# A GeGLU MLP kernel: in the two down phases that make w_down operands, block loads moved ahead of the transposes of x, and their first sums moved later

## The chip, the cores and the metric

One NeuronCore of a Trainium2 chip runs the whole kernel. The metric is the device time of one execution in microseconds (us). Most executions agree within 0.3%. Profiles are of one execution each.

## The reference, cut to what matters

```python
gate = x @ w_gate                       # x: 8 x 1024 x 1024, weights 1024 x 4096
up = x @ w_up
gate = 0.5 * gate * (1 + np.tanh(np.sqrt(2 / np.pi) * (gate + 0.044715 * gate ** 3)))
h = gate * up
return (h @ w_down).astype(np.float32)  # w_down: 4096 x 1024
```

## The kernel before

The kernel works in 8 passes of 1024 tokens, numbered 0 to 7. Each has a gate/up phase and a down phase. The first passes use a Strassen-like scheme with 7 products (P1 to P7), the later ones a deeper one with 24 operands, whose w_down combinations are made once, in "units", beside other work, and stored in DRAM. The down phases of passes 2 and 3 carry two units each. A down phase of this kind has 14 chunks of w_down operands, 1 MB each, and 4 groups of rows per chunk: 56 *slots* of 8 matmuls, numbered from 0. A unit reads *blocks* of w_down, 256 KB each, sums and scales them, and stores the results.

In the profiles TensorE is PE (the matmuls), VectorE is DVE (here the sums), ScalarE is ACT (here copies and scaled copies); SyncE (SP) and GpSimd (POOL) issue DMA transfers. PSUM is the memory in banks that takes the matmuls' sums; the *ring* holds the chunks on the core. A transfer *lands* when its data has arrived. The *granted clock* is the share of TensorE's full clock that the profile reports. The parts that matter:

```python
def down(p):
    ...
    steps = {}
    if p in UNITS_DOWN:                       # passes 2 and 3, two units each
        free = deque(xc[:, j * 512 : (j + 1) * 512] for j in range(24, 38))   # 14 buffers
        for i, u in enumerate(UNITS_DOWN[p]):
            load, fs = wd_unit(u, xc[:, i * 8192 : i * 8192 + 4096], free)
            steps[i] = [load]                 # 3 loads on SyncE, 1 casting load on GpSimd
            for k, f in enumerate(fs):        # 20 steps: store, sum (VectorE), scaled copy (ScalarE)
                steps.setdefault(3 + 19 * i + k, []).append(f)
    ...
    for v, name in enumerate(DSEQ):           # P1 P2 P6 P5 P7 P3 P4
        for nb in range(2):
            kc = 2 * v + nb                   # chunk
            dc = d_chunk(p, kc)
            for g in range(G):                # slot (2 * v + nb) * 4 + g
                for n in range(8):
                    nc.tensor.matmul(ps_all[:, bank[b, g]], lhs[:, j, g * P : (g + 1) * P], dc[:, n, :], ...)
                ...
                if nb == 1:
                    if name == "P1":          # slots 4 to 7: P2 adds to this copy from slot 8
                        bank["c", g] = ps_free.popleft()
                        nc.scalar.copy(ps_all[:, bank["c", g]], ps_all[:, bank["a", g]])
                    ...
                for s in sums.get((name, nb, g), ()):
                    hsum(*s)
                ...
                if nb == 0 and g == 0 and p + 1 < NPASS:
                    ...
                    if v == (2 if p < FAST - 1 else 0):
                        transpose_x(p + 1)    # four DMA transposes on SyncE's queue
                for f in steps.get((2 * v + nb) * G + g, ()):
                    f()
                ...
            if kc == 0 and p < FAST:          # FAST is 3: in pass 2, not in pass 3
                for k in range(3, 6):
                    load_d(p, k)              # chunks 3, 4, 5, on SyncE
            load_d(p, kc + 6)
```

In the timelines SyncE issues its DMAs in program order (in pass 2 before the change: transposes at 796.08 us, blocks at 811.92, chunks at 815.36). Chunks 0 to 2 of pass 2, and 0 to 5 of pass 3, are issued during the gate/up phase.

## Time and profile before

| | |
|---|---|
| time, median of the first 3 runs | 2293.49 us (2290.92 to 2293.87) |
| TensorE busy | 2257.8 us of 2289.5 us |
| TensorE waits for the PSUM copy, passes 2 and 3 | 9.9 + 8.3 us |
| down phase of pass 0, pass 2, pass 3 | 96.7, 108.3, 106.8 us |

The core's time is the sum of TensorE's phases, one after the other. A phase's length against the 96.7 us that its 448 matmuls take without a wait tells what it loses. The prediction below shows the lines.

### The profile page before, as it was taken

Reading aid. Unit: us, or ns where it says so; the run is one execution under the profiler, and the core shown is the slowest. Engines: PE = TensorE matmul, PEld = TensorE weight load, DVE = VectorE, ACT = ScalarE, POOL = GpSimd, SP = SyncE. Lnnn points to the kernel's source line nnn. Section 1 sums busy time; section 2 is a strip of 40 time slices with the busy share of each in tenths; the row PEclk is TensorE's granted clock in tenths of the full one; section 3 lists DMA queues with packets and bytes.
Section 4 is the critical chain, followed back from the end, with each engine's and each line's share of the span. In section 5 each row is a group of like instructions: output and inputs, shape, how many; then the busy total and the mean of one; then the engine's idle time right before and its main releaser. Section 6 shows DMA issues by size and latency. Waiting matters only on the chain.

```text
span 2289.5 us, 42138 instructions
## 1 busy us (share of the span) xinstructions
PE 2257.8 (99%) x16255; PEld 1589.1 (69%) x16255; DVE 1524.7 (67%) x2170; ACT 959.3 (42%) x1876; POOL 687.8 (30%) x826
## 2 busy tenths in 40 slices
PE   9999999999999989999899999999999999999999
PEld 4444444444444435888358888888888888888888
DVE  5576368772587744877548777766776767866674
ACT  4443135551355522665216651255503554045520
POOL 1342013230133300555105541154502544034520
PEclk9999999999999999999999999999999999999999
DMA  9998959888899999998989999998999989998876
GB/s 239 175 210 209 252 145 223 216 255 248 184 220 223 265 301 300 326 379 294 290 270 326 389 323 305 333 304 291 300 321 320 319 275 305 332 312 275 285 287 231
DMA packets 305306, 632.98 MB, mean 276 GB/s; under 512 B 78992, under 2 KB 181392, under 8 KB 285840
## 3 DMA queue, kind: packets, MB, share of 16 engines
q1 hardware_dynamic: 250048, 556.88, 71.3%
q0 software_dynamic: 55056, 73.41, 19.3%
q8 instruction: 127, 2.08, 0.4%
q14 instruction: 75, 0.61, 0.1%
HBM read 565.18 MB, written 138.41 MB: 307 GB/s over the span
## 4 chain that ended last, share of the span: by engine, by line
PE 93%; DMA 3%; DVE 2%; SPq 1%; issue 1%; ACT 0%; DVEq 0%; ACTq 0%
PE ps L827 38%; PE ps L620 22%; PE ps L965 16%; PE ps L1079 16%; DMA ring<-w_ops 1%; DVE ring L349 1%; SPq L254 1%; DMA h_s<-wd_ops 1%; PE ps L1178 1%; DVE x_sums L277 0%; DMA x_sums<-wd_ops 0%; DVE tmp L639 0%; DMA h_a<-in_x_dram 0%; DVE h_a L657 0%; DVE h_s L410 0%
## 5 line engine op out<-in xcount | busy, mean ns | idle before, releaser
L827 PEld LDWEIGHTS <-ring 128*128 128x128 f16 x8320 | 814.1, 98 | 97.8 <-issue 3.2
L804 POOL TENSOR_TENSOR h_a<-tmp 128x256 f16<-128x256 f32 x640 | 472.5, 758 | 787.3 <-ACT tmp L792 774.6
L827 PE MATMUL ps<-x_sums,ring 128*128 128x256 f16 x5760 | 655.9, 273 | 0.2 <-DVE tmp L789 0.2
L789 DVE TENSOR_TENSOR tmp<-tmp,ps 128x512 f32<-128x512 f32 x640 | 414.4, 683 | 147.7 <-PE ps L827 103.3
L620 PEld LDWEIGHTS <-ring 128*128 128x128 f16 x2632 | 257.5, 98 | 314.8 <-issue 5.1
L774 ACT COPY tmp<-ps 128x512 f32<-128x512 f32 x520 | 303.5, 585 | 219.6 <-PE ps L827 146.6
L620 PE MATMUL ps<-x_sums,ring 128*128 128x512 f16 x1504 | 341.1, 379 | 3.1 <-DVE ring L349 1.7
L792 ACT ACTIVATE tmp<-tmp 128x256 f32<-128x256 f32 x640 | 263.3, 417 | 175.6 <-DVE tmp L787 81.6
L965 PE MATMUL ps<-ring,h_a 128*128 128x512 f16 x1408 | 308.9, 382 | 18.2 <-ACT ps L981 18.2
L827 PE MATMUL ps<-x_b,ring 128*128 128x256 f16 x2560 | 305.9, 273 | 2.5 <-DVE tmp L789 2.5
L965 PEld LDWEIGHTS <-h_a 128*128 128x128 f16 x1536 | 150.9, 98 | 202.0 <-issue 22.8
L646 POOL TENSOR_TENSOR h_a<-tmp 128x512 f16<-128x512 f32 x94 | 148.9, 1584 | 377.4 <-ACT tmp L644 288.4
L787 DVE TENSOR_TENSOR tmp<-ps,tmp 128x512 f32<-128x512 f32 x240 | 165.4, 689 | 143.0 <-ACT tmp L774 98.7
L620 PE MATMUL ps<-x_b,ring 128*128 128x512 f16 x1128 | 259.1, 379 | 0.0
L639 DVE TENSOR_TENSOR tmp<-ps,tmp 128x512 f32<-128x512 f32 x188 | 127.1, 684 | 135.6 <-ACT tmp L631 132.7
L1079 PEld LDWEIGHTS <-h_a 128*128 128x128 f16 x1792 | 175.4, 98 | 20.3
L1079 PE MATMUL ps<-ring,h_a 128*128 128x256 f16 x1536 | 172.9, 273 | 0.0
L1136 ACT ACTIVATE tmp<-ps 128x512 f32<-128x512 f32 x48 | 28.2, 597 | 290.1 <-PE ps L1079 219.7
L893 ACT ACTIVATE tmp<-ps 128x512 f32<-128x512 f32 x64 | 38.2, 597 | 265.9 <-PE ps L965 265.9
L631 ACT COPY tmp<-ps 128x512 f32<-128x512 f32 x188 | 110.1, 586 | 91.8 <-PE ps L620 89.3
L349 DVE TENSOR_TENSOR ring<-ring 128x1024 f16<-128x1024 f16 x188 | 132.8, 721 | 7.2 <-PE ps L965 3.8
L644 ACT ACTIVATE tmp<-tmp 128x512 f32<-128x512 f32 x94 | 58.8, 626 | 147.5 <-DVE tmp L639 147.4
(94 smaller groups left out, 1557.5 us busy)
## 6 DMA issues: line engine op xcount, KB each, us to landing
ring<-w_ops SPq DMA_DIRECT2D x480, 512.0 KB, 5.1
ring<-wd_quads SPq DMA_DIRECT2D x88, 1024.0 KB, 7.3
ring<-wd_ops SPq DMA_DIRECT2D x49, 1024.0 KB, 7.8
out_dram<-tmp SPq DMA_DIRECT2D x128, 256.0 KB, 6.2
w_ops<-x_sums SPq DMA_DIRECT2D x110, 256.0 KB, 6.2
ring<-in_w_gate_dram POOLq DMA_DIRECT2D x23, 1024.0 KB, 9.1
ring<-in_w_up_dram POOLq DMA_DIRECT2D x23, 1024.0 KB, 17.3
w_ops<-h_s SPq DMA_DIRECT2D x82, 256.0 KB, 5.1
```

What stands on the lines that cost most here:

```text
L349: nc.vector.tensor_tensor(o, a, b, op)
L620: nc.tensor.matmul(ps(b, w), lhs[:, k], rhs[:, k, :], start=(first and k == 0), stop=(k == KH - 1), skip_group_check=True,)
L639: nc.vector.tensor_tensor(o, ps("b", w), o, ADD)
L646: nc.gpsimd.tensor_tensor(hq[TO[n]][:, i, :], tmp[:, t[n, 1]], tmp[:, t[n, 0]], MUL)
L774: nc.scalar.copy(tmp[:, t[o[1]]], ps_all[:, bank[o[2]]])
L787: nc.vector.tensor_tensor(d, b, a, SUB)
L789: nc.vector.tensor_tensor(d, a, b, ADD if o[4] == "add" else SUB)
L792: nc.scalar.activation(d, d, GELU, scale=GSC)
L804: nc.gpsimd.tensor_tensor(h, tmp[:, t[o[1]], MQ : 2 * MQ], g, MUL)
L827: nc.tensor.matmul(ps_all[:, bank[c], w * MQ : (w + 1) * MQ], lhs[:, w, k], rhs[:, k], start=(first and w == 0 and k == 0), stop=(k == KH ...
L965: nc.tensor.matmul(ps_all[:, bank[b, g]], lhs[:, j, g * P : (g + 1) * P], dc[:, n, :], start=(first and j == 0), stop=(j == NP - 1), skip_ ...
L1079: nc.tensor.matmul(ps_all[:, bank[c], m * MQ : (m + 1) * MQ], lhs[:, j, m * P : (m + 1) * P], rhs[:, j, :], start=(first and j == 0 and m ...
```

## The change

The intent is that the unit's blocks are there when ScalarE's first scaled copy asks for them, and that this copy stands behind the PSUM copies in any case.

```diff
                 load, fs = wd_unit(u, xc[:, i * 8192 : i * 8192 + 4096], free)
-                steps[i] = [load]
+                steps.setdefault(0, []).append(load)
                 for k, f in enumerate(fs):
-                    steps.setdefault(3 + 19 * i + k, []).append(f)
+
+                    steps.setdefault(9 + (17 if i else 0) + 5 * k // 6, []).append(f)
...
                     for s in sums.get((name, nb, g), ()):
                         hsum(*s)
+                    for f in steps.get((2 * v + nb) * G + g, ()):
+                        f()
                     if p == 0:
...
                             transpose_x(p + 1)
-                    for f in steps.get((2 * v + nb) * G + g, ()):
-                        f()
```

## The prediction

> **What bounds the kernel now.** I read the page first. The third line below names the instruction groups that carry the chain.
>
> ```profile
> PE 2257.8 (99%) x16255; PEld 1589.1 (69%) x16255; DVE 1524.7 (67%) x2170; ACT 959.3 (42%) x1876; POOL 687.8 (30%) x826
> ...
> PE 93%; DMA 3%; DVE 2%; SPq 1%; issue 1%; ACT 0%; DVEq 0%; ACTq 0%
> PE ps L827 38%; PE ps L620 22%; PE ps L965 16%; PE ps L1079 16%; DMA ring<-w_ops 1%; DVE ring L349 1%; SPq L254 1%; DMA h_s<-wd_ops 1%; PE ps L1178 1%; DVE x_sums L277 0%; DMA x_sums<-wd_ops 0%; DVE tmp L639 0%; DMA h_a<-in_x_dram 0%; DVE h_a L657 0%; DVE h_s L410 0%
> ```
>
> TensorE is busy 99% of 2289.5 us. This change removes no matmul, so it can pay only through the 1% in which TensorE waits. The view of waits, for TensorE alone, shows how that splits; columns are total, times, longest:
>
> ```profile
> PE ps L965 <- ACT ps L981: 18.2, 2, 9.9
> PE ps L827 <- DVE tmp L789: 2.7, 3, 1.4
> PE ps L620 <- DVE ring L349: 1.7, 4, 0.4
> ```
>
> One line dominates: two waits in the down matmuls (L965), for the copy by ScalarE of a partial sum from one PSUM bank to another (L981). Two waits, and two phases that make w_down operands (passes 2 and 3): that is what the change is after. The chain in order of time (start, length, what) gives the phases' lengths. The first line is pass 0's down phase, with none of this work; the next three are from pass 2, the last two from pass 3:
>
> ```profile
> 213.73 96.69 PE ps L965 x448
> ...
> 796.00 13.83 PE ps L965 x64
> ...
> 819.10 0.59 ACT ps L981
> 819.73 84.60 PE ps L965 x384
> ...
> 1109.44 0.49 ACT ps L981
> 1109.98 84.54 PE ps L965 x384
> ```
>
> A clean phase is 448 matmuls in 96.69 us: 56 steps ("slots") of 8 matmuls, 1.727 us each. Pass 2 takes 904.32 (where the next phase's piece starts) - 796.00 = 108.32 us, 11.6 over clean. Pass 3 takes 1194.52 - 1087.73 (its first down matmul in the timeline) = 106.79, 10.1 over. Together 21.7 us, 0.95% of the time: the ceiling of the change.
>
> Why ScalarE is late, from the timeline of pass 2 (start, length, engine, line; the bracket is the idle time before it and what ended it):
>
> ```profile
> 796.08 15.79 SPq L254 DMA_TRANSPOSE x_b<-x_half  x4
> ...
> 811.92 3.33 SPq L470 DMA_DIRECT2D x_sums<-wd_ops  x6
> 815.36 2.51 SPq L529 DMA_DIRECT2D ring<-wd_ops  x4
> ...
> 818.56 0.63 ACT L500 ACTIVATE x_sums<-x_sums 128x512 f16<-128x512 f16 x1 [21.69 <-DMA x_sums<-wd_ops]
> ...
> 819.10 1.55 ACT L981 COPY ps<-ps 128x512 f32<-128x512 f32 x3
> 819.73 10.57 PE L965 MATMUL ps<-ring,h_a 128*128 128x512 f16 x41 [9.91 <-ACT ps L981]
> ```
>
> SyncE's one queue issues the four transposes of x for 15.8 us, then the loads of w_down blocks. In ScalarE's order, the first scaled copy of a block (L500, slot 3) stands ahead of the PSUM copies (L981, slots 4 to 7), so they wait for its load and TensorE for them. Windows of 4 us show a second cost (PE busy is the second number; granted clock follows POOL):
>
> ```profile
> 812.00:816.00 4.00, 0.00 (x0) 0.00 (x0) 0.57 (x2) 0.00 (x0) 0.00 (x0) 0.58 1.10 220
> ...
> 820.00:824.00 4.00, 4.00 (x13) 1.52 (x12) 4.00 (x7) 2.24 (x5) 0.00 (x0) 0.64 1.00 421
> 824.00:828.00 4.00, 4.00 (x21) 1.79 (x19) 3.97 (x7) 0.00 (x0) 0.00 (x0) 1.00 1.02 424
> ```
>
> After the wait TensorE restarts at half clock (13 matmuls in 4 us, then 21). So pass 2's excess is 9.9 of wait + 1.7 of slow restart, pass 3's 8.3 + 1.8.
>
> **What the Trainium skill says.** "TensorE: Matmul & The Clock Gate" (Part 1, The two states you'll see): the clock falls to half after an idle window of about 3.4 us and returns after about as long busy. Here it fell about 2.8 us after TensorE stopped at 809.8 (full until about 812.6) and was back at about 823, 3.2 us after the restart; it agrees roughly. The same page (Architectural detail) calls ScalarE a strict FIFO, as the trace shows: ready copies sat behind L500. "Perfetto Trace Analysis" (Summary: the profiler window per engine type) says a DMA's profiled interval on a hardware queue is its issue and hides the data movement; so I add the landing time. Here the six loads issue in 3.3 us and land 3.4 to 7.4 us after issue.
>
> **The change part by part.** It adds and removes no work; it reorders.
>
> (a) Both units' loads (six on SyncE, 3.3 us to issue; two casting loads on GpSimd) now go ahead of the transposes. SyncE reaches them at 796.1; the last is issued at about 799.4 and lands within 7.4 us, by about 807.
>
> (b) The first sums and scaled copies move from slot 3 to slot 9. In ScalarE's order all four PSUM copies (slots 4 to 7) now come first. I compared the instruction orders: in the two phases L981 is x4 with nothing between. Slot 9 ends some 17 us into the phase, about 813, after the loads. Both causes of the two waits are removed: -11.6 and -10.1.
>
> (c) The transposes move back by the loads' 3.3 us. Whatever follows them on SyncE keeps its time: it still stands behind 15.8 + 3.3 us of issue. In pass 2 that is L529: w_down chunks 3, 4, 5 and 6 of the down phase itself. Chunk 3 is first read in slot 12. Before, TensorE reached slot 12 late, at 819.73 + 6.9 = 826.6, and chunk 3 (issued 815.36, landed 8.9 us later) was there at 824.3: 2.3 us to spare. The old wait covered this one. Now TensorE reaches slot 12 at 795.84 + 12 x 1.727 = 816.6, and chunk 3 is still issued at 796.08 + 3.3 + 15.8 + gaps = 815.3. Its landing should be quicker, with no block loads in front: in pass 1 a chunk issued right after the transposes landed 6.0 us later (a different stretch of the schedule, but the same 1 MB). So 821.3, and a new wait of about 4.7 us. That is longer than the 2.8 us at which the clock fell, so add 1.7 for a slow restart: 6.4 us. Chunk 4 follows some 2.5 us later (before, chunks 3 and 4 landed 2.5 us apart) and is needed a further 6.9 us on: no wait. Pass 2 keeps 11.6 - 6.4 = 5.2.
>
> (d) In pass 3 chunks 0 to 5 are issued during gate/up, the last at 1087.9, before the transposes. Only chunk 6 comes behind them (1105.84 before), needed in slot 24, at 1087.7 + 41.4 = 1129. No new wait: pass 3 keeps 10.1.
>
> (e) The second unit's 20 steps now take slots 26 to 41 rather than 22 to 41: 1.2 sums per slot. A sum is 0.43 us on VectorE; that is 0.1 us more per slot. VectorE idled 7.1 us (pass 2) and 13.7 us (pass 3) just before the add at slot 36 that frees a bank for slot 40. Covered.
>
> Sum: -5.2 - 10.1 = -15.3 us; 2293.5 - 15.3 = 2278.
>
> **The rivals.**
> 1. Everything is recovered, 21.7 us: 2272. For it: the two waits are the only large ones. Against: chunk 3. The transposes would have to issue in 10 us rather than 15.8; other passes show 13.1 to 19.7.
> 2. The chunk wait eats pass 2's whole gain: 2283. It needs a wait of 10 us. The 1.5 MB of block loads now lie in the queue ahead of the transposes and could slow them by some us, and with 19.7 us of transposes, as in pass 0, chunk 3 lands at 825.2. Half plausible.
> 3. Contention later: denser stores stop VectorE on its 14 buffers until the add of slot 36 is late. Pass 2 has 16.5 us of waits on those stores in VectorE, yet none reached TensorE. It would cost 2 to 5 us: 2281 to 2283.
> 4. Transposes too late for the scaling and sums of x from slot 32: they land at about 820, slot 32 comes after 851. Ruled out.
>
> **Range and chances.** The floor is 2272, the likely mishaps end near 2284, and the three runs of before spread over 3 us: 2271 to 2284 holds it 8 times in 10. A gain over 2% (46 us) is twice the ceiling: 0.01. A loss over 2% would need a new wait of 46 us plus the gain: 0.005.
>
> **What would show it.** Right: the waits of L965 for L981 are gone; the pass 3 phase is about 97 us; in pass 2 one TensorE wait of 3 to 7 us at slot 12, 21 us into the phase, for the DMA into the ring (or put down to "issue"), and a dip in granted clock after it; the phase some 103 us. Wrong: no TensorE gap at slot 12 (rival 1), one near 10 us (2), or gaps around slot 40 (3). A pass 3 phase well over 97 us would mean that I missed a load there.

## The result, and the profile after

The changed kernel takes 2277.94 us (median of 4 runs, 2275.76 to 2280.97); before, in the rounds of the same comparison, 2292.20 us. The ratio is 0.9939, interval 0.9922 to 0.9956: 0.6% faster. Added lines move line numbers by one: L966 is the down matmul that was L965, L982 the PSUM copy that was L981.

TensorE's largest wait in the changed kernel (total, times, longest); the next is 1.7 us in total:

```profile
PE ps L966 <- DMA ring<-wd_ops: 5.4, 1, 5.4
```

The 18.2 us of waits for ScalarE are gone. In their place stands one wait of 5.4 us for a load of w_down operands into the ring. The chain in order of time says where:

```profile
795.30 13.83 PE ps L966 x64
...
814.84 6.54 DMA ring<-wd_ops
...
821.42 77.77 PE ps L966 x352
899.19 54.16 PE ps L827 x496
...
1082.96 96.69 PE ps L966 x448
```

Pass 2's phase is 899.19 - 795.30 = 103.9 us, 7.2 over clean, where it was 11.6 over. Pass 3's is one piece of 96.69 us. The gain of the two phases is 4.4 + 10.1 = 14.5 us; the medians differ by 14.3, the two profiled spans (2289.5 and 2273.7) by 15.8. The timeline of pass 2 shows the order of events:

```profile
795.37 3.52 SPq L470 DMA_DIRECT2D x_sums<-wd_ops  x6
...
798.99 15.75 SPq L254 DMA_TRANSPOSE x_b<-x_half  x4
...
803.97 0.57 ACT L982 COPY ps<-ps 128x512 f32<-128x512 f32 x1 [7.80 <-PE ps L966]
...
809.64 1.15 ACT L500 ACTIVATE x_sums<-x_sums 128x512 f16<-128x512 f16 x2
...
814.84 3.14 SPq L529 DMA_DIRECT2D ring<-wd_ops  x5
...
821.42 8.91 PE L966 MATMUL ps<-ring,h_a 128*128 128x512 f16 x33 [5.40 <-DMA ring<-wd_ops]
```

The PSUM copies run as soon as TensorE has their sums, and the first scaled copies come after the fourth of them. The ring loads (L529) still stand behind the transposes, at 814.84, and slot 12, which TensorE reaches at 816.0, needs the first of them. Windows of 2 us show the half clock after the wait (second number PE busy; the granted clock is the third from the end):

```profile
820.00:822.00 2.00, 0.58 (x2) 0.25 (x2) 0.00 (x0) 0.00 (x0) 0.00 (x0) 0.83 1.00 422
822.00:824.00 2.00, 2.00 (x7) 0.65 (x5) 0.00 (x0) 0.00 (x0) 0.00 (x0) 0.50 1.02 430
824.00:826.00 2.00, 2.00 (x9) 0.82 (x8) 0.00 (x0) 0.60 (x1) 0.00 (x0) 0.81 1.00 422
```

It costs 7.2 - 5.4 = 1.8 us. One more line, from the waits of pass 2's down phase: VectorE now waits longer for free buffers, 30.4 us against 16.5, but no TensorE wait came from it.

```profile
DVE x_sums L277 <- DMA wd_quads<-x_sums: 30.4, 8, 14.9
```

### The profile page after: what moved, and what is told of

Read it like the earlier page. It is cut to its first block, busy times and chain, and to the rows that moved or that the text cites. A ratio compares the mean times of both kernels' runs of the same rounds, so it can differ in the third digit from the quotient of the medians.

```text
span 2273.7 us, 42142 instructions
## 1 busy us (share of the span) xinstructions
PE 2255.4 (99%) x16255; PEld 1587.4 (70%) x16255; DVE 1522.1 (67%) x2170; ACT 959.7 (42%) x1876; POOL 688.1 (30%) x826
## 4 chain that ended last, share of the span: by engine, by line
PE 94%; DMA 3%; DVE 2%; issue 0%; SPq 0%; ACT 0%; DVEq 0%; ACTq 0%
PE ps L827 37%; PE ps L620 23%; PE ps L966 17%; PE ps L1080 16%; DMA ring<-w_ops 2%; DMA h_s<-wd_ops 1%; PE ps L1179 1%; DVE ring L349 1%; DMA h_a<-in_x_dram 0%; DMA ring<-wd_ops 0%; DVE x_sums L277 0%; SPq L254 0%; DVE tmp L639 0%; DVE h_a L657 0%; DVE h_s L410 0%
## 5 line engine op out<-in xcount | busy, mean ns | idle before, releaser
L966 PE MATMUL ps<-ring,h_a 128*128 128x512 f16 x1408 | 307.3, 381 | 5.4 <-DMA ring<-wd_ops 5.4
L966 PEld LDWEIGHTS <-h_a 128*128 128x128 f16 x1536 | 150.5, 98 | 188.0 <-issue 7.9
```

## The experiments

The theory: all that the two phases lost, before and after, comes from what stands behind the 15 us of transposes on SyncE's queue. Before, that was the block loads; the wait for them also hid that the chunk loads of pass 2 were late. Eight runs were made in two groups of five rounds, four in each; all gave correct results. The first group holds the two halves of the change and the first tries of chunks first, on either kernel; the second holds the changed kernel again, chunks first again, and the two runs with later transposes. Each group shares its runs of the kernel before, and the groups ran on different chips (13 and 4 in the record). The kernel before took 2293.72 us (median of 11 runs) in the first group and 2291.87 in the second, so across groups the ratios are to be compared, not the times.

**The loads alone.** The changed kernel with the sums back in their old slots:

```diff
-                    steps.setdefault(9 + (17 if i else 0) + 5 * k // 6, []).append(f)
+                    steps.setdefault(3 + 19 * i + k, []).append(f)
```

> Half of the change alone: the block loads go ahead of the transposes of x, but the sums keep their old slots (3 to 22 and 22 to 41), so the first scaled copy still stands ahead of the PSUM copies on ScalarE. My theory (the copy waited for the late load, not for its place in the order as such): the block it reads is issued about 1 us into the phase and lands some 5 us later, about when the copy's turn comes (slot 3, 5 to 7 us in), so the PSUM copies are in time for slot 8 at 13.8 us: no wait of the down matmuls for ScalarE, the pass 3 phase is 97 us, pass 2 again has its wait of 5 to 6 us for chunk 3 in slot 12 and takes about 104 us. Time about 2278 us, ratio to before 0.9935 to 0.9945, as the whole change. Rival (the place in ScalarE's order is what counts): waits of several us for the PSUM copies remain in both phases, and the time lies between 2283 and 2292 us.

Measured: 2278.90 us, ratio 0.9939 (0.9924 to 0.9953). TensorE's waits have the same single large line (5.5 us for the ring load), pass 2's phase is 900.57 - 795.86 = 104.7 us, pass 3's 96.69. ScalarE in pass 2:

```profile
802.51 0.63 ACT L500 ACTIVATE x_sums<-x_sums 128x512 f16<-128x512 f16 x1 [5.78 <-DMA x_sums<-wd_ops]
804.53 0.57 ACT L982 COPY ps<-ps 128x512 f32<-128x512 f32 x1 [1.39 <-PE ps L966]
```

The scaled copy still stands first and still waits for its load, but the load comes in time: the PSUM copy then waits for TensorE, not TensorE for it. With the blocks early, the place in the order alone did no harm.

**The late sums alone.** The kernel before with only the slots changed; the loads stay behind the transposes:

```diff
-                    steps.setdefault(3 + 19 * i + k, []).append(f)
+                    steps.setdefault(9 + (17 if i else 0) + 5 * k // 6, []).append(f)
```

> The other half alone: the sums come at slots 9 to 24 and 26 to 41, but the block loads stay behind the transposes. My theory: the PSUM copies now stand ahead of the late scaled copy, so the waits for ScalarE go; the pass 3 phase is 97 us. In pass 2 the chunk loads still stand behind the transposes and now also behind the six block loads, so chunk 3 lands about 8.9 us after its issue at 19.5 us into the phase, 28.4 us in, against 20.7 us needed: a wait of 7 to 8 us for it in slot 12, 2 us more than in the whole change; the phase is about 106 us. Time about 2280 to 2281 us, ratio 0.9945 to 0.9955. Rival (late blocks now stop VectorE before the sums of h that the products of slot 16 read): a second wait in slot 16, in pass 3 too, and a time of 2284 us or more.

Measured: 2279.83 us, ratio 0.9946 (0.9932 to 0.9961). The waits for ScalarE are gone here too: the PSUM copies now run before the scaled copy, whose load is as late as before. ScalarE in pass 2, and the chain of this kernel:

```profile
805.79 0.57 ACT L981 COPY ps<-ps 128x512 f32<-128x512 f32 x1 [7.80 <-PE ps L965]
...
818.03 1.15 ACT L500 ACTIVATE x_sums<-x_sums 128x512 f16<-128x512 f16 x2 [6.49 <-DMA x_sums<-wd_ops]
```

```profile
797.12 13.83 PE ps L965 x64
...
815.61 8.36 DMA ring<-wd_ops
...
824.01 77.61 PE ps L965 x352
901.62 52.41 PE ps L827 x480
...
1087.33 96.69 PE ps L965 x448
```

The chunk takes 8.36 us to land, behind the six block loads, against 6.54 in the changed kernel; 8.9 was expected. The wait is only 6.2 us, less than the 7 to 8 expected: the chunk was issued some 18.5 us after the phase's start, not 19.5, since the transposes issued in 14.2 us. Pass 2's phase is 104.5 us, pass 3's 96.69, and no wait came at slot 16. So either half of the change removes both waits; the two gains are not added but are the same gain. The times of the halves cannot be told from the whole: the intervals overlap.

**The changed kernel again**, as the control of the second group (chunks first again, and the two runs with later transposes):

> The changed kernel again, as the control in the same rounds as the next three. Expected as recorded: about 2278 us, ratio to before 0.992 to 0.9955, pass 2's down phase 103 to 105 us with one wait of 5 to 6 us for chunk 3, pass 3's 96.7 us. If the profiles differ elsewhere, it is in the stretch before pass 2's down phase, where runs of the same schedule have differed by up to 3 us.

Measured: 2279.47 us, ratio 0.9942 (0.9930 to 0.9954). Its profile has a chunk wait of 6.2 us, where 5 to 6 were expected, a pass 2 phase of 900.36 - 794.48 = 105.9 us, somewhat over the 103 to 105 expected, and a pass 3 phase of 96.69. The slow restart cost more here: 352 matmuls took 78.92 us where clean they take 352 x 0.2158 = 75.97, so 2.9 us against 1.8. The windows show why; the clock was at half for longer:

```profile
824.00:826.00 2.00, 2.00 (x6) 0.69 (x5) 0.00 (x0) 0.60 (x1) 0.00 (x0) 0.50 1.01 426
826.00:828.00 2.00, 2.00 (x8) 0.83 (x7) 0.00 (x0) 0.12 (x1) 0.00 (x0) 0.72 1.01 360
```

**Chunks 3 to 5 ahead of the transposes, on the changed kernel.**

```diff
                 if nb == 0 and g == 0 and p + 1 < NPASS:
...
+                    if v == 0 and p == FAST - 1:
+                        for k in range(3, 6):
+                            load_d(p, k)
                     if v == (2 if p < FAST - 1 else 0):
                         transpose_x(p + 1)
...
-            if kc == 0 and p < FAST:
+            if kc == 0 and p < FAST - 1:
```

> The whole change, and in pass 2 the loads of chunks 3, 4 and 5 are issued ahead of the transposes as well. My theory (chunk 3's place behind the transposes is all that is left of the loss): the wait in slot 12 goes, the granted clock does not dip in the phase, and the pass 2 phase is 96.7 to 97.5 us against 103.9 in the changed kernel. Time 2270 to 2272 us, ratio 0.990 to 0.991; faster than the changed kernel by 6 to 7 us. Rival (the wait only moves, since transposes that now stand behind 3 MB more of loads hold up the operand stores and chunk 6 behind them): a new wait at slot 24 or at the start of pass 3's gate/up, and no more than 3 us gained over the changed kernel.

Measured: 2274.41 us, ratio 0.9915 (0.9901 to 0.9930). Pass 2's phase is one piece, free of waits, so the wait is removed and did not move:

```profile
798.05 96.69 PE ps L966 x448
```

In the same rounds this is 4.5 us below the loads alone, whose profile lost 8.0 us in pass 2. But the time was some 3 us over what was expected, and the phase had started 2.7 us later than in the changed kernel's profile. So it ran again beside the control:

> The changed kernel with chunks 3 to 5 of pass 2 ahead of the transposes, again: its first profile had a pass 2 phase of 96.7 us with no wait, but its time was only 3.5 us below that of the changed kernel (in other rounds), where 7 were expected; the profile had started that phase 2.7 us later. My theory (that delay is scatter of the executions and not of the kernel): in the same rounds as the control it is 5 to 8 us faster than the changed kernel, about 2271 to 2272 us, and the pass 2 phase does not start later than the control's by more than 1 us. Rival (the change costs something elsewhere): again only 2 to 4 us faster, with 2 us or more lost in the gate/up phase after it.

Measured: 2270.14 us, ratio 0.9901 (0.9889 to 0.9914), 9.3 us below the control's median. The phase started at 794.96, 0.5 us after the control's. The later start of the first try was thus not the kernel's doing: up to there the programs of all ten profiles are the same, and this phase starts between 794.5 and 798.1 us in them. Whether the chip or the execution made it late is not settled; three of the first try's four runs took 2274.4 to 2274.6 us, so it was not one stray execution. The gain over the control is larger than the 5 to 8 expected, since this control's profile lost 9.2 us in pass 2 rather than 7. TensorE's timeline in that phase (the bracket is the wait before a piece):

```profile
794.80 55.42 PE L966 MATMUL ps<-ring,h_a 128*128 128x512 f16 x256
...
866.59 26.06 PE L966 MATMUL ps<-ring,h_a 128*128 128x512 f16 x120 [0.84 <-DVE tmp L897]
```

A small wait is new: 0.84 us just after slot 40, for VectorE's add (L897). VectorE had stood waiting for buffers in front of it. The first try did not have it.

**Chunks 3 to 5 ahead of the transposes, on the kernel before.** The same edit without the change:

> The kernel before, with only the loads of chunks 3, 4 and 5 of pass 2 put ahead of the transposes. My theory (before the change, chunk 3's lateness was hidden behind the wait for ScalarE): no gain at all; the block loads come 1 to 2 us later, so the wait for the PSUM copies in pass 2 grows from 9.9 to about 11 to 12 us. Time 2292 to 2296 us, ratio 0.999 to 1.002. Rival (chunk 3 was already part of the loss in the kernel before): the pass 2 phase gets shorter by 2 us or more and the time falls below 2290 us.

Measured: 2298.32 us, ratio 1.0021 (1.0006 to 1.0035), slightly slower, and above the 2292 to 2296 expected. SyncE's timeline, and the waits:

```profile
795.44 1.59 SPq L529 DMA_DIRECT2D ring<-wd_ops  x3
797.14 18.64 SPq L254 DMA_TRANSPOSE x_b<-x_half  x4
815.82 2.96 SPq L470 DMA_DIRECT2D x_sums<-wd_ops  x6
```
```profile
PE ps L965 <- ACT ps L981: 23.1, 2, 14.2
```

The block loads came some 4.5 us later in the phase, not 1 to 2, because the transposes took 18.6 us to issue behind the chunk loads; the wait in pass 2 grew from 9.9 to 14.2 us and not to 12. The edit that gained 4.5 to 9.3 us with the blocks early gains nothing on the kernel before. It is not a clean test of chunk 3 there, since it also delayed the blocks, which is enough to explain the loss (4.3 us more wait in pass 2, 4.6 us by the medians). That chunk 3 did not bind the kernel before is read from its waits: in pass 2 TensorE waited only for the copies.

**The transposes later, on the kernel before.** One thing is moved, and the sums keep their slots:

```diff
-                    if v == (2 if p < FAST - 1 else 0):
+                    if v == (2 if p < FAST - 1 else 0) and p not in UNITS_DOWN:
                         transpose_x(p + 1)
+                if v == 0 and nb == 1 and g == 0 and p in UNITS_DOWN and p + 1 < NPASS:
+                    transpose_x(p + 1)
```

> The kernel before with one thing moved: in passes 2 and 3 the transposes are issued from slot 4 on, behind the block loads and the chunk loads; the sums keep their old slots. My theory (all that was lost in the two phases was lost to the transposes' 15 us ahead of the loads on one queue): both phases take 96.7 to 98 us, no wait for ScalarE and none for chunk 3, and the time is 2270 to 2273 us, ratio 0.990 to 0.9915, some 6 us better than the changed kernel. Rival (the sums at their old slots, now with early blocks and stores held up behind the transposes, run out of buffers and stop VectorE or ScalarE): a wait at slot 16 or later of 2 us or more in each phase, and a time above 2275 us.

Measured: 2272.29 us, ratio 0.9912 (0.9899 to 0.9925). There is no wait in either phase, and each takes 96.69 us; pass 2's in the chain, and SyncE's order in its timeline:

```profile
795.53 96.69 PE ps L965 x448
```
```profile
795.60 3.59 SPq L470 DMA_DIRECT2D x_sums<-wd_ops  x6
799.30 3.49 SPq L529 DMA_DIRECT2D ring<-wd_ops  x4
803.18 21.32 SPq L254 DMA_TRANSPOSE x_b<-x_half  x4
```

This is the theory's plainest test: nothing but the transposes moved, and all of the two phases' loss went (19.6 us by the medians, of the 21.7 counted). They now take 21.3 us to issue in pass 2, and no TensorE wait in the phase comes from it.

**The transposes later, on the changed kernel.** The same edit on top of the change:

> The changed kernel with the transposes issued from slot 4 on in passes 2 and 3: block loads, chunk loads, then the transposes, and the late sums. My theory: as the run with chunks 3 to 5 first, both phases 96.7 us, 2270 to 2273 us, and within 1.5 us of the kernel before with only the transposes moved: the late sums add nothing once the loads are early. Rival (the late sums matter once the stores stand behind the transposes): 2 us or more faster than the one with old slots.

Measured: 2273.15 us (2267.74 to 2277.53), ratio 0.9912 (0.9898 to 0.9927), the same ratio as without the late sums. Its profile has a wait of 1.1 us for L897 in pass 2, as in the second run of chunks 3 to 5 first; pass 3's phase is 96.69. No gain from the late sums is seen once the loads are early; the intervals are too wide to exclude one of 2 us. With chunks first the median was lowest, 2270.14 us, but its interval overlaps with those of these two; which of the three is best is not settled.

## Why the prediction was right

The prediction was 2278 us and the result 2277.94. Step by step:

- **(a) and (b), the two waits go.** Right. No wait for L982 is left, and either half alone does it; the prediction named both parts together and did not see that one is enough.
- **(c), the new wait in slot 12 of pass 2.** Right in place and cause. Chunk 3 was issued 19.7 us into the phase (814.84 - 795.14), predicted 19.5. It landed in 6.5 us, predicted 6.0, and the wait was 5.4 us, predicted 4.7; in the control 7.1 and 6.2. The slow restart cost 1.8 us, predicted 1.7, and 2.9 in the control. Pass 2 in the first profile kept 4.4 us of the predicted 5.2, and 2.4 (11.6 - 9.2) in the control. The term that was sized low is the wait with its restart: 7.2 and 9.2 us against 6.4. Two of its side sums are off. In the kernel before, it had TensorE reach slot 12 at 826.6 us and left out its own slow restart of 1.7 us: it was about 828.3, so chunk 3 had some 4 us to spare, not 2.3. And for rival 1 the transposes would have had to issue in about 11 us (15.8 - 4.7), not 10. Neither changes the forecast.
- **That the old wait covered the new one** is shown by the halves of the change: each removes only the wait for ScalarE, and in each the wait for chunk 3 appears (5.5 and 6.2 us). Chunks first agrees, with no gain before the change and 4.5 to 9.3 us after it.
- **(d), pass 3.** Right: 96.69 us, all 10.1 us kept, in the profile of every run in which the waits for ScalarE went.
- **(e), VectorE's margin.** Right for the changed kernel, where VectorE still idled 5.6 us before the add of slot 36. The new wait may have helped: with that removed, two of the three such profiles with the late, denser sums have a wait of 0.8 or 1.1 us for that add or the next, and the one with the old slots has none. That the denser sums cause it is likely, not shown.
- **The rivals.** The full recovery (2272) did not come, and for the reason given; it came as soon as the order on the queue was mended. The second rival's mechanism, loads ahead that slow the issue of the transposes, is real but struck elsewhere: in pass 3 they took 22.3 us in the changed kernel (18.2 in the control) against 14.5 before, where nothing near was waiting; in pass 2 it was 15.75 against 15.79. The third showed as more VectorE waiting without effect on the end.

The near-exact total is partly luck. The gain was 14.3 us, not 15.3, and the kernel before took 2292.2 us in these rounds, not 2293.5; the two errors cancel. The control's median lay 1.5 us higher, and single executions of one kernel spread by 5 to 10 us.

## What to carry to other kernels

When a wait is removed, ask what else was late at that moment: a load that arrives in time (here by some 4 us) may have its margin only thanks to the wait, and the next thing on the same queue may become the new wait. Long issues on an in-order queue (here transposes) belong behind the loads that are needed first; moving the one long item behind all of them gained 20 us, moving the block loads and chunks 3 to 5 ahead of it 19 and 22, and moving only the block loads ahead of it some 14. Two remedies for one wait do not add up: try each alone.

## What the Trainium skill lacked or had wrong

- "DMA: Bandwidth & Descriptors" (Latency and other measured facts) gives DMA transposes an effective 261 GB/s, or more when contiguous, but I found on no page the time for which transposes of this size hold the issuing queue. Here four transposes of 0.5 MB (2.1 MB in all) held SyncE for 11.7 to 22.6 us, 93 to 180 GB/s by issue time. In pass 2 it was 18.6 to 22.6 us in the five profiles with chunk loads in front of them and 14.2 to 16.4 in the five without, six block loads in front or not; yet pass 0, with only stores just in front, took 19.1 to 21.7. What sets it is not settled.
- "TensorE: Matmul & The Clock Gate" (Part 1) has the clock fall after an idle window of about 3.4 us and return after about as long busy, and has the point of change vary by 0.5 us either way. Here, in eight waits of 5.4 to 14.2 us, it fell 2.4 to 5.3 us after TensorE stopped and returned 3.0 to 5.7 us after it went on, a wider spread, and the slow restart cost 1.6 to 2.9 us on top of the wait. The moments are worked out from the granted clock in windows of 1 to 4 us, taken as full or half: 0.83 in the window 820 to 822 above puts the fall at 821.3.
- I found it on no page that a wait can hide a late load on the same queue: with either half of the change the wait of 9.9 us for ScalarE in pass 2 went, and one of 5.5 or 6.2 us for a chunk behind the same transposes appeared.
